# An expert loop with its gathers and additions spread out, and an end with other operations

## The chip, the core and the metric

The kernel runs on one core of a Trainium2 chip. A core has TensorE (matrix products, written PE in the profile, its weight loads PEld), VectorE (DVE), ScalarE (ACT), GpSimd (POOL) and SyncE (SP), which here issues nearly all transfers from the chip's main memory (HBM) into the on-chip memory (SBUF). Matrix products land in eight PSUM banks. Measured is the time of one execution in microseconds (us), the median of several.

## The reference

A two-layer backbone on 256 latent tokens of width 1024 and 256 context tokens. Each layer mixes the tokens in four parallel branches and then applies a channel mixer; in the second layer this is a choice of 2 out of 8 experts, whose weights (8 x 3 matrices of 1024 x 3584 in float32) are most of what is read:

```python
def moe_swiglu(h, router, w1, w3, w2):
    logits = (h @ router).astype(jnp.float32)
    top_v, top_i = lax.top_k(logits, TOP_K)
    probs = jax.nn.softmax(top_v, axis=-1)
    combine = jnp.sum(jax.nn.one_hot(top_i, N_EXPERTS, dtype=jnp.float32) * probs[..., None], axis=-2).astype(h.dtype)
    out = jnp.zeros_like(h)
    for e in range(N_EXPERTS):
        out = out + combine[..., e:e + 1] * swiglu(h, w1[e], w3[e], w2[e])
    return out
# in the layer: x = x + g2 * moe_swiglu(h2, ...), and at the very end
# return rmsnorm(x, final_norm_g)
```

## The kernel before

The first layer and the second layer's mixer take some 815 us; the change touches only what follows, the experts.

**Routing.** `last_proj` finishes the residual `res` in two tiles of 128 tokens; for each, `finish` computes the router's logits `lg` and the normalized tokens `H` in two parts, H1 (rounded to float32r, the fast matmul type) and the remainder H2. `route` ranks the logits and finds each token's place in its expert's list (`pos`); its inner function `weights` makes the softmax weights `comb`. `by_load` sorts the experts by their number of tokens: expert 0 stays first, the three fullest of the others are "heavy" (128 slots, computed with split float32r products: `split` makes two parts of each weight unit, a cast on ScalarE, L145, and a subtraction on VectorE, L146), the other four and expert 0 are "light" (64 slots, plain float32 on the raw weights). It also reads the experts' numbers into SP's registers, for the addresses of their weights.

**Gathering.** `one_hot` builds P from position and choice; `gather` multiplies H by P in eight column blocks (L1058), each evicted by ScalarE and VectorE into XE (heavy) or XL (light), through two PSUM banks of the tag "sm"; `turned` transposes P to PT for the way back. A call serves one heavy and one light expert. For a light expert P and Q hold the one-hots beside zeros, so that PT has 128 rows for each half.

**The loop** in `moe` goes through 56 steps, 21 heavy and 35 light: seven chunks of 512 hidden columns for each expert. The first four steps are light ones of expert 0 (`lead`), then heavy and light ones are mixed evenly. A step reads six weight units of 1 MiB: w1 and w3 in two halves each (`moe_first`, `light_first`) and w2 in two (`moe_second`, `light_second`, called later, after the transpose of the activation, `turns`). Inside a step, between units, stand calls that interleave other work: `look_ahead` splits a coming unit, and `heavy_aside` or `light_aside` run one part of a gather (`run(side, 1)`), the transposes, the second product, or the additions. Within the loop the order of every compute engine is the program's order, written out by a chain of dependencies at the end of `moe`; ahead of it a planner orders the work.

**Adding.** After an expert's last chunk `scatter` or `light_scatter` multiplies the result by the gate `g2`, splits it in two float32r parts Y1 and Y2, and later four `put`s follow: each multiplies PT by Y1 and Y2 (L1208, L1209) and adds the product, times the token's weight, to half a tile of `res` (L1211).

**Buffers.** SP loads units into ten buffers in turn (L119) and waits for each until its last reader is done. With four more units in the split's tiles and three in tiles that are free until later, seventeen are loaded ahead of the loop's first product. `final` normalizes `res` and writes the output.

Of the kernel before, what the change touches and what calls it, by code (L numbers as in the profile page):

```python
# [49 lines left out]
class Net:  # L50
    def __init__(self, tc, d, dump=None):
# [18 lines left out]
        self.hact, self.hpool = (1,), (1,)  # L70
# [873 lines left out]

    def route(self):
# [3 lines left out]
        lg, sel, oh1, oh2 = self.lg, T("sel"), T("oh1"), T("oh2")  # L949
        big = E.tile([128, 2, 2, 8, 8], F32, tag="P", name="big", bufs=1)  # L950
        gt, ge = (big[:, i] for i in range(2))
        selb = E.tile([128, 2, 8], BF16, name="selb")
        rank = T("rank")
        for t in range(2):
            mine = lg[:, t, :, None].to_broadcast([128, 8, 8])
            other = lg[:, t, None, :].to_broadcast([128, 8, 8])
            V.tensor_tensor(ge[:, t], other, mine, op=ALU.is_equal)
            V.tensor_tensor(ge[:, t], ge[:, t], self.low, op=ALU.mult)
            V.tensor_tensor(gt[:, t], other, mine, op=ALU.is_gt)
            V.tensor_tensor(gt[:, t], gt[:, t], ge[:, t], op=ALU.add)  # L960
            V.tensor_reduce(rank[:, t], gt[:, t], axis=AX.X, op=ALU.add)
            V.tensor_scalar(selb[:, t], rank[:, t], 1.5, None, op0=ALU.is_lt)
            V.tensor_scalar(sel[:, t], rank[:, t], 1.5, None, op0=ALU.is_lt)
# [32 lines left out]
        self.comb, self.sel, self.pos, self.tmp = comb, sel, pos, tmp  # L996
        self.dbg("pos", pos)

    def by_load(self):
# [31 lines left out]
        self.placed.append(table("combS", self.comb))  # L1031
# [18 lines left out]
    def gather(self, P, XE=None, XL=None):  # L1050
# [3 lines left out]
        for k in range(8):  # L1054
# [10 lines left out]
            if XL is not None:  # L1065
                nc.scalar.activation(XL[:, k], pg[:, o:], AF.Identity, bias=sh, scale=A)
# [15 lines left out]
    def moe_first(self, src, XE, c, aside=lambda n: None):  # L1082
# [3 lines left out]
        for n, name in enumerate(("m_w1", "m_w3")):  # L1086
            ps = self.bank(tag="mm")
            for kh in range(2):
# [8 lines left out]
                self.look_ahead()  # L1097
                aside(2 * n + kh)
# [89 lines left out]
    def scatter(self, PT, y, cmb):  # L1188
# [16 lines left out]
    def put(self, t, s, PT, Y1, Y2, cmb):  # L1205
        nc = self.nc
        ps = self.bank(tag="mm")
        nc.tensor.matmul(ps, PT, Y1, start=True, stop=False)  # L1208
        nc.tensor.matmul(ps, PT, Y2, start=False, stop=True)  # L1209
# [3 lines left out]
    def light_scatter(self, PT, y, cmb):  # L1213
        nc = self.nc
        Y = self.O.tile([128, 2, 1024], F32R, tag="Y", name=self.nm("Y"))
        Y1, Y2, yg = Y[:, 0, :512], Y[:, 1, :512], self.t2()
        for hf in range(2):
            p = slice(64 * hf, 64 * hf + 64)
            nc.vector.tensor_tensor(yg[p], y[p], self.g2[p, 512 * hf:512 * hf + 512], op=ALU.mult)
# [3 lines left out]
        for t in range(2):  # L1223
            for hf in range(2):
                self.put(t, slice(512 * hf, 512 * hf + 512), PT[:, t, hf], Y1, Y2, cmb)
# [4 lines left out]
    def moe(self):  # L1230
# [3 lines left out]
        def tables(i):  # L1234
            tabs = (self.pos, self.sel, self.comb) if i == 0 else self.placed
            return [a[:, :2, i:i + 1] for a in tabs]

        def light(i, P):

            Q = E.tile([128, 2, 128], F32R, tag="Q", name=self.nm("Q"), bufs=1)  # L1240
            nc.vector.memset(P[:, :, 192:].bitcast(F32), 0.0)
            nc.vector.memset(Q[:, :, :64].bitcast(F32), 0.0)
            pos, sel, _ = tables(i)
            self.one_hot(P[:, :, 128:192], pos, sel)
            self.one_hot(Q[:, :, 64:], pos, sel)
            XE[i] = E.tile([128, 8, LCAP], F32, tag="XL", name=self.nm("XL"), bufs=2)
            PT[i] = E.tile([128, 2, 2, 128], F32R, tag="PTL", name=self.nm("PTL"), bufs=2)
            return Q

        def heavy(i, P):  # L1250
            pos, sel, _ = tables(i)
            self.one_hot(P[:, :, :128], pos, sel)
            XE[i], PT[i] = self.xe_tile(), self.pt_tile()

        def turn(i, P, Q=None):
            if Q is None:
                self.turned(PT[i], [P[:, t, :128] for t in range(2)])
            else:
                self.turned(PT[i].rearrange("p t h c -> p (t h) c"), [x for t in range(2) for x in (P[:, t, 128:], Q[:, t])])

        def gather(i, j):
# [4 lines left out]
            Q = light(j, P)  # L1266
            yield from self.gather(P[:, :, 0 if i else 128:192], XE.get(i), XE[j])
            if i:
                turn(i, P)
            turn(j, P, Q)  # L1270
# [16 lines left out]
        run(side, 9)  # L1287
# [22 lines left out]

        def second(kind, **kw):

            while todo[kind] and todo[kind][0] in G:
# [4 lines left out]
                if c == EFF_CH - 1:  # L1318
                    late.append((self.scatter if kind else self.light_scatter)(PT[i], y[i], tables(i)[2]))
# [15 lines left out]
        for m, (i, c) in enumerate(steps):  # L1335
            kind = big(i)
            if i == 0 and c == 4:
# [3 lines left out]
                nc.scalar.dma_start(self.fg, self.d["fng"])  # L1341
            if c == 0 and i not in ready:
# [4 lines left out]
            def light_aside(n):  # L1347
                if n == 1:
                    turns(False)
                if n == 3 and big(after[0]):  # L1350
# [9 lines left out]
                elif n == 3 and todo[True] and not any(big(x) for x, _ in steps[m:]):  # L1360
# [388 lines left out]
```

## Time and profile before

| | us |
|---|---|
| median of 3 runs | 1694.98 (1692.75 to 1695.25) |
| the profiled execution, time | 1690.82 |
| its span, first to last instruction | 1689.1 |
| busy: TensorE | 1608.9 (95%) |
| busy: VectorE, ScalarE, GpSimd | 955.9, 679.7, 35.4 |
| read from HBM | 478.86 MB |
| mean granted clock of TensorE | 0.976 |

The profile is of one execution. Start times in the rows count from the span's start. Matmuls are pipelined: the duration of one is longer than the distance to the next, and the distance is what a row of them costs. A float32 product appears as two records. The granted clock is a share of the full 2.4 GHz. "Idle before" stands in brackets with what ended it.

### The profile page before, as it was taken

How to read it: one execution, taken by the hardware profiler on the slowest of the kernel's cores; microseconds unless marked ns; L12 is line 12 of the kernel's file. 1: busy time of each engine (PE TensorE's matmuls, PEld its weight loads, DVE VectorE, ACT ScalarE, POOL GpSimd, SP SyncE). 2: the span in 40 equal slices, each digit the busy share in tenths (PEclk: the TensorE clock that was granted, in tenths of full speed). 3: DMA queues.
4: the chain of work that ended last, by engine and by line, in shares of the span. 5: the costliest groups of instructions: out<-in, count | busy, mean ns of one | idle time of the engine just before them, and what ended most of it. 6: DMA issues, size and time to landing. Idle time of an engine off the chain costs nothing. (4 is left out here: it accounts for less than half of the span.)

```text
span 1689.1 us, 23700 instructions
## 1 busy us (share of the span) xinstructions
PE 1608.9 (95%) x9333; PEld 1202.3 (71%) x9333; DVE 955.9 (57%) x1455; ACT 679.7 (40%) x1086; POOL 35.4 (2%) x46
## 2 busy tenths in 40 slices
PE   6999999999999999999899999999999999999986
PEld 3878799887787878999656766666676666775653
DVE  3769655567565688588314554447454454545343
ACT  4654244422222226765314434344343343533341
POOL 1000000000000030000000000000000000000000
PEclk9999999999999999999798999999999999999997
DMA  9544441535443542325898999999999999999994
GB/s 363 195 164 150 180 162 51 184 140 189 160 174 138 207 154 101 125 76 205 335 417 315 419 418 413 405 418 419 418 395 398 419 420 412 418 419 419 419 420 168
DMA packets 69030, 481.55 MB, mean 285 GB/s; under 512 B 8064, under 2 KB 8192, under 8 KB 12336
## 3 DMA queue, kind: packets, MB, share of 16 engines
q1 hardware_dynamic: 68480, 479.43, 71.5%
q8 instruction: 75, 1.23, 0.3%
q10 hardware_dynamic: 432, 0.54, 0.1%
q14 instruction: 43, 0.35, 0.1%
HBM read 478.86 MB, written 1.08 MB: 284 GB/s over the span
## 5 line engine op out<-in xcount | busy, mean ns | idle before, releaser
L146 DVE TENSOR_TENSOR s<-raw,s 128x1024 fp32r<-128x1024 f32 (+1 forms) x350 | 414.9, 1221 | 272.2 <-ACT s L145 271.6
L145 ACT CAST s<-raw 128x1024 fp32r<-128x1024 f32 (+1 forms) x350 | 355.4, 1050 | 277.6 <-PE mm L181 98.0
L176 PE MATMUL mm<-X,s 128*128 128x512 f32 (+1 forms) x672 | 247.2, 368 | 0.0
L181 PE MATMUL mm<-X,s 128*128 128x512 f32 (+1 forms) x672 | 247.0, 368 | 0.0
L182 PE MATMUL mm<-X,s 128*128 128x512 f32 (+1 forms) x672 | 245.8, 368 | 0.0
L1157 PE MATMUL mm<-raw,XL 128*64 128x256 f32 x1952 | 218.9, 380 | 0.6 <-DMA raw<-in_m_w_dram 0.6
L1157 PEld LDWEIGHTS mm<-raw,XL 128*64 128x64 f32 x1952 | 138.7, 137 | 82.6 <-issue 15.9
L176 PEld LDWEIGHTS mm<-X,s 128*128 128x128 f32 x672 | 126.4, 188 | 27.9 <-issue 6.7
L181 PEld LDWEIGHTS mm<-X,s 128*128 128x128 f32 x672 | 126.7, 189 | 26.0 <-issue 5.9
L182 PEld LDWEIGHTS mm<-X,s 128*128 128x128 f32 x672 | 126.6, 189 | 24.0 <-issue 3.4
L176 PE MATMUL mm<-s,XE 128*128 128x512 f32 x336 | 139.2, 414 | 2.2 <-ACT s L145 2.1
L181 PE MATMUL mm<-s,XE 128*128 128x512 f32 x336 | 136.4, 406 | 2.0 <-DVE s L146 2.0
L182 PE MATMUL mm<-s,XE 128*128 128x512 f32 x336 | 135.9, 404 | 0.0
L1184 PE MATMUL yl<-raw,GL 128*64 128x512 f32 x488 | 110.5, 597 | 0.5 <-ACT GL L1172 0.5
L1161 ACT ACTIVATE t<-mm 128x256 f32<-128x256 f32 x35 | 13.5, 386 | 218.9 <-PE mm L1157 218.9
L176 PE MATMUL mm<-s,X 128*128 128x256 f32 (+1 forms) x304 | 86.5, 287 | 2.0 <-ACT mix L666 2.0
L181 PE MATMUL mm<-s,X 128*128 128x256 f32 (+1 forms) x304 | 86.0, 285 | 0.8 <-DVE s L146 0.8
L1163 DVE TENSOR_TENSOR t<-t,mm 128x256 f32<-128x256 f32 x35 | 14.6, 417 | 125.0 <-PE mm L1157 124.9
L182 PE MATMUL mm<-s,X 128*128 128x256 f32 (+1 forms) x304 | 85.1, 285 | 0.0
L1184 PEld LDWEIGHTS yl<-raw,GL 128*64 128x64 f32 x488 | 33.0, 137 | 63.6 <-issue 62.0
L176 PEld LDWEIGHTS mm<-s,XE 128*128 128x128 f32 x336 | 65.6, 195 | 17.3 <-ACT s L145 3.1
L181 PEld LDWEIGHTS mm<-s,XE 128*128 128x128 f32 x336 | 65.5, 195 | 17.4 <-DVE s L146 3.1
(384 smaller groups left out, 2347.7 us busy)
## 6 DMA issues: line engine op xcount, KB each, us to landing
raw<-in_m_w_dram SPq DMA_DIRECT2D x294, 1024.0 KB, 14.0
mraw<-in_mod_w_dram SPq DMA_DIRECT2D x47, 1024.0 KB, 4.9
raw<-in_f_w_dram SPq DMA_DIRECT2D x33, 1024.0 KB, 5.0
mraw<-in_m_w_dram SPq DMA_DIRECT2D x32, 1024.0 KB, 12.4
raw<-in_w_in_dram SPq DMA_DIRECT2D x20, 1024.0 KB, 4.8
raw<-in_w_out_dram SPq DMA_DIRECT2D x8, 1024.0 KB, 5.6
first<-in_m_w_dram SPq DMA_DIRECT2D x8, 512.0 KB, 9.0
once<-in_m_w_dram SPq DMA_DIRECT2D x3, 1024.0 KB, 16.1
```

What stands on the lines that cost most here:

```text
L145: self.last = (nc.scalar.copy(s1[:, :h], r), nc.vector.tensor_tensor(s2[:, :h], r, s1[:, :h].bitcast(F32), op=ALU.subtract))
L146: nc.vector.tensor_tensor(s2[:, :h], r, s1[:, :h].bitcast(F32), op=ALU.subtract))
L176: m = mm(out, a[0], b[0], start=first, stop=False)
L181: self.keep(mm(out, a[0], b[1], start=False, stop=False))
L182: self.keep(mm(out, a[1], b[0], start=False, stop=last))
L1157: self.keep(nc.tensor.matmul(ps[64 * b:64 * b + 64], XL[:, k], w(o, o + 256), start=(k == 0), stop=(k == 7), tile_position=(0, 64 * b)))
L1161: nc.scalar.activation(g, ps, AF.Silu)
L1163: self.keep(nc.vector.tensor_tensor(g, g, ps, op=ALU.mult))
L1184: self.keep(self.nc.tensor.matmul(y[64 * hf:64 * hf + 64], G[:, b, 64 * hb:64 * hb + 64], w(o, o + 512), start=(c == 0 and hb == b == 0), ...
```

## The change

1. `rank_of` is cut out of `route` and called in `finish` for each tile of tokens as its logits are there; the subtraction for H2 of the second tile goes from GpSimd to VectorE (`hpool`).
2. `weights` and the table of the sorted weights, `combS`, move from ahead of the loop into its second step.
3. A gather now first makes its one-hots and yields; ahead of the loop these are made for experts 1 and 4 too, and the eight parts of that gather run in light steps 1 to 3, three per step. Later gathers make their one-hots as soon as they are set up. In the first gather every second eviction goes to VectorE.
4. For light experts P holds the one-hots twice and Q is gone; the additions use 64 rows of the array (`tile_position`) for each half.
5. `heavy_aside` does one `put` per call in place of four in two calls; in `moe_first` the aside goes ahead of `look_ahead`, but for the second.
6. After the last heavy step its transposes and additions move into the first half of the next light step.
7. The light gate is laid out in `g2l` and applied in one multiplication; the last expert's additions take the result in float32, without the split.
8. `final` multiplies by the norm's weight ahead of the scale, so that after the root one operation remains.

```diff
-        self.hact, self.hpool = (1,), (1,)
+        self.hact, self.hpool = (1,), ()
...
             if XL is not None:
-                nc.scalar.activation(XL[:, k], pg[:, o:], AF.Identity, bias=sh, scale=A)
+                if o == 0 and k % 2:
+                    nc.vector.tensor_scalar(XL[:, k], pg, A, sh, op0=ALU.mult, op1=ALU.add)
+                else:
+                    nc.scalar.activation(XL[:, k], pg[:, o:], AF.Identity, bias=sh, scale=A)
...
-                self.look_ahead()
-                aside(2 * n + kh)
+                if 2 * n + kh == 1:
+                    self.look_ahead()
+                    aside(1)
+                else:
+                    aside(2 * n + kh)
+                    self.look_ahead()
...
-                self.put(t, s, PT[:, t], Y1[:, s], Y2[:, s], cmb)
+                self.put(t, s, PT[:, t], (Y1[:, s], Y2[:, s]), cmb)
+                yield
...
+        yg = self.t2()
+        nc.vector.tensor_tensor(yg, y, self.g2l, op=ALU.mult)
+        if last:
+            for t in range(2):
+                for hf in range(2):
+                    p = slice(64 * hf, 64 * hf + 64)
+                    self.put(t, slice(512 * hf, 512 * hf + 512), PT[p, t].bitcast(F32), (yg[p],), cmb, tile_position=(64 * hf, 0))
+            return
...
         def gather(i, j):
             P = E.tile([128, 2, 256], F32R, tag="P", name=self.nm("P"), bufs=1)
             if i:
                 heavy(i, P)
-            Q = light(j, P)
+            light(j, P)
+            yield
...
         def begin():
             yield from gather(None, 0)
-            self.weights()
             self.by_load()
-            yield
             yield from gather(1, NH + 1)
...
-        run(side, 9)
+        run(side, 10)
...
         def heavy_aside(n):
             if n == 1:
                 turns(False)
-                puts()
+                put()
                 second(True, aside=lambda: run(side, 1))
-            elif n == 3:
-                puts()
+            else:
+                put()
             run(side, 1)
...
+            if i == 0 and c == 1:
+                self.weights()
+                self.combS = self.table("combS", self.comb)
...
-            def light_aside(n):
-                if n == 1:
+            def light_aside(k):
+                if k == 1:
                     turns(False)
-                if n == 3 and big(after[0]):
+                    if not any(big(x) for x, _ in steps[m:]):
+                        turns(True)
+                        puts()
+                    if 0 < m < n:
+                        run(side, 3)
+                if k == 3 and big(after[0]):
...
                 side = gather(*more[i, c])
+                run(side, 1)
...
+            r = self.rms(ss, t)
+            for hf in range(2):
+                s = slice(512 * hf, 512 * hf + 512)
+                nc.vector.tensor_tensor(both[:, t, s], self.res[t][:, s], self.fg[:, s], op=ALU.mult)
             for hf in range(2):
...
-                if self.fmode and hf < self.fmode:
-                    nc.scalar.activation(o, self.res[t][:, s], AF.Copy, scale=rt)
-                    nc.vector.tensor_tensor(o, o, self.fg[:, s], op=ALU.mult)
+                if hf == 0:
+                    nc.scalar.activation(o, o, AF.Copy, scale=r)
                 else:
-                    nc.vector.scalar_tensor_tensor(o, self.res[t][:, s], rt, self.fg[:, s], op0=ALU.mult, op1=ALU.mult)
+                    nc.vector.tensor_scalar(o, o, r, None, op0=ALU.mult)
```

## Rows read from the trace of the kernel before

**Rows 1.** The page, transfer rate (GB/s) in 40 slices of the span.
```profile
GB/s 363 195 164 150 180 162 51 184 140 189 160 174 138 207 154 101 125 76 205 335 417 315 419 418 413 405 418 419 418 395 398 419 420 412 418 419 419 419 420 168
```

**Rows 2.** By stretches: length, busy us per engine, granted clock, transfer share, GB/s.
```profile
828.00:1672.00 844.00, 803.60 (x4680) 537.70 (x4678) 388.24 (x459) 324.86 (x442) 0.00 (x0) 0.97 0.98 401
832.00:848.00 16.00, 16.00 (x130) 9.39 (x128) 0.84 (x2) 1.04 (x3) 0.00 (x0) 0.97 0.63 235
888.00:920.00 32.00, 29.31 (x148) 18.39 (x150) 12.38 (x15) 13.15 (x20) 0.00 (x0) 0.85 0.76 280
1040.00:1440.00 400.00, 382.59 (x2234) 262.05 (x2233) 201.41 (x242) 164.63 (x226) 0.00 (x0) 0.98 1.00 411
1440.00:1660.00 220.00, 208.51 (x1181) 138.41 (x1181) 99.49 (x101) 83.82 (x105) 0.00 (x0) 0.98 1.01 419
1660.00:1664.00 4.00, 4.00 (x40) 2.70 (x38) 0.00 (x0) 0.38 (x1) 0.00 (x0) 1.00 0.37 146
```

**Rows 3.** Timeline ahead of the loop: start, us, engine, line, out<-in, count [idle before].
```profile
814.95 0.23 DVE L1586 SCALAR_TENSOR_TENSOR lg<-sm,rstd,shR 128x8 f32<-128x8 f32 x1 [0.77 <-PE sm L1608]
...
816.26 2.49 POOL L1596 TENSOR_TENSOR H<-t,H 128x512 fp32r<-128x512 f32 x2 [1.45 <-ACT t L1592]
...
816.52 1.03 DVE L962 TENSOR_SCALAR selb<-rank 128x8 bf16<-128x8 f32 x1
...
819.72 2.84 PE L1058 MATMUL sm<-P,H 128*128 128x64 f32 x12 [0.67 <-DVE P L1047]
...
821.46 1.28 ACT L977 ACT_TABLE_LOAD   x1
...
828.63 9.28 PE L1157 MATMUL mm<-first,XL 128*64 128x256 f32 x64
...
839.68 0.33 SPq L119 DMA_DIRECT2D mraw<-in_m_w_dram  x1
```

**Rows 4.** Timeline of TensorE, gather of experts 1 and 4, first heavy chunk.
```profile
879.91 1.14 PE L1058 MATMUL sm<-P,H 128*128 128x192 f32 x8
...
892.97 0.79 PE L176 MATMUL mm<-s,XE 128*128 128x512 f32 x1 [1.62 <-ACT s L145]
...
895.25 0.63 PE L176 MATMUL mm<-s,XE 128*128 128x512 f32 x1
895.67 0.63 PE L181 MATMUL mm<-s,XE 128*128 128x512 f32 x1
...
898.54 0.39 PE L176 MATMUL mm<-s,XE 128*128 128x512 f32 x1
898.77 0.40 PE L181 MATMUL mm<-s,XE 128*128 128x512 f32 x1
```

**Rows 5.** Waits, 905 to 1660: engine, line <- releaser: us, times, longest.
```profile
PE mm L1208 <- DVE res L1211: 12.2, 4, 3.1
...
PE sm L1058 <- DVE P L1047: 9.7, 3, 3.4
...
PE y L176 <- ACT G L1120: 5.0, 1, 5.0
...
PE sm L1073 <- ACT XL L1066: 4.6, 2, 2.3
```

**Rows 6.** Timeline, two float32 products of 512 columns.
```profile
870.43 1.98 PE L365 MATMUL mod<-mrow,ident 128*128 128x512 f32 x4
```

**Rows 7.** Timeline of the end.
```profile
1641.00 1.99 ACT L145 CAST s<-raw 128x1024 fp32r<-128x1024 f32 x2 [4.69 <-DMA raw<-in_m_w_dram]
...
1672.60 1.39 DVE L1219 TENSOR_TENSOR t<-yl,gf 64x512 f32<-64x512 f32 x2 [3.19 <-PE yl L1184]
...
1676.01 3.07 DVE L1211 SCALAR_TENSOR_TENSOR res<-mm,combS,res 128x512 f32<-128x512 f32 x4 [0.59 <-PE mm L1209]
...
1681.95 0.72 ACT L1662 ACTIVATE out<-res,rstd 128x512 f32<-128x512 f32 x1 [1.17 <-POOLq L1403]
...
1682.70 0.69 DVE L1663 TENSOR_TENSOR out<-out,gf 128x512 f32<-128x512 f32 x1
```

More of the change, by code (lines that the diff above doesn't have):

```diff
@@ L942, in ffn, with rank_of @@
         second(DFF_CH - 1, prev)
+    def rank_of(self, t):
+        nc, V, lg = self.nc, self.nc.vector, self.lg
+        gt, ge = (self.t2((128, 8, 8), tag="t1") for _ in range(2))
+        mine = lg[:, t, :, None].to_broadcast([128, 8, 8])
+        other = lg[:, t, None, :].to_broadcast([128, 8, 8])
+        V.tensor_tensor(ge, other, mine, op=ALU.is_equal)
+        V.tensor_tensor(ge, ge, self.low, op=ALU.mult)
+        V.tensor_tensor(gt, other, mine, op=ALU.is_gt)
+        V.tensor_tensor(gt, gt, ge, op=ALU.add)
+        V.tensor_reduce(self.rank[:, t], gt, axis=AX.X, op=ALU.add)
+        V.tensor_scalar(self.selb[:, t], self.rank[:, t], 1.5, None, op0=ALU.is_lt)
+        V.tensor_scalar(self.sel[:, t], self.rank[:, t], 1.5, None, op0=ALU.is_lt)
     def route(self):
@@ L948, in route @@
         T = lambda nm, *sh: E.tile([128, 2, 8, *sh], F32, name=nm)
[L949 to L963, printed above, removed]
+        lg, sel, selb, rank, oh1, oh2 = self.lg, self.sel, self.selb, self.rank, T("oh1"), T("oh2")
         m = E.tile([128, 4, 2], F32, name="mx")
@@ L1202, in scatter, with put, light_scatter @@
                 s = slice(512 * hf, 512 * hf + 512)
-                self.put(t, s, PT[:, t], Y1[:, s], Y2[:, s], cmb)
-    def put(self, t, s, PT, Y1, Y2, cmb):
+                self.put(t, s, PT[:, t], (Y1[:, s], Y2[:, s]), cmb)
+                yield
+    def put(self, t, s, PT, Y, cmb, **kw):
         nc = self.nc
         ps = self.bank(tag="mm")
-        nc.tensor.matmul(ps, PT, Y1, start=True, stop=False)
-        nc.tensor.matmul(ps, PT, Y2, start=False, stop=True)
+        for i, y in enumerate(Y):
+            nc.tensor.matmul(ps, PT, y, start=(i == 0), stop=(i == len(Y) - 1), **kw)
         a = self.res[t][:, s]
         nc.vector.scalar_tensor_tensor(a, ps, cmb[:, t], a, op0=ALU.mult, op1=ALU.add)
-    def light_scatter(self, PT, y, cmb):
+    def light_scatter(self, PT, y, cmb, last=False):
         nc = self.nc
+        yg = self.t2()
[6 more added lines that the diff above has]
+            return
         Y = self.O.tile([128, 2, 1024], F32R, tag="Y", name=self.nm("Y"))
[L1216 to L1219, printed above, removed]
+        Y1, Y2 = Y[:, 0, :512], Y[:, 1, :512]
         nc.scalar.copy(Y1, yg)
@@ L1224, in light_scatter @@
             for hf in range(2):
-                self.put(t, slice(512 * hf, 512 * hf + 512), PT[:, t, hf], Y1, Y2, cmb)
+                p = slice(64 * hf, 64 * hf + 64)
+                self.put(t, slice(512 * hf, 512 * hf + 512), PT[p, t], (Y1[p], Y2[p]), cmb, tile_position=(64 * hf, 0))
+                yield
     def ys(self):
@@ L1309, in puts, with put @@
                 run(late.pop(0))
+        def put():
+            if late and next(late[0], self) is self:
+                late.pop(0)
         def second(kind, **kw):
@@ L1318, in second @@
                 if c == EFF_CH - 1:
+                    puts()
+                    if kw.get("last"):
+                        run(self.light_scatter(PT[i], y[i], tables(i)[2], True))
+                        return
                     late.append((self.scatter if kind else self.light_scatter)(PT[i], y[i], tables(i)[2]))
@@ L1341, in moe @@
                 nc.scalar.dma_start(self.fg, self.d["fng"])
+                self.g2l = E.tile([128, 512], F32, name="g2l")
+                for hf in range(2):
+                    nc.scalar.copy(self.g2l[64 * hf:64 * hf + 64], self.g2[64 * hf:64 * hf + 64, 512 * hf:512 * hf + 512])
             if c == 0 and i not in ready:
@@ L1359, in light_aside @@
                         self.plan[2:2] = [(source(i)("m_w2", c, hb), 1) for hb in range(2)]
-                elif n == 3 and todo[True] and not any(big(x) for x, _ in steps[m:]):
+                elif k == 3 and todo[True] and not any(big(x) for x, _ in steps[m:]):
                     i, c = todo[True][0]
                     self.plan = [(source(i)("m_w2", c, hb), 1) for hb in range(2)]
-                if n == 3:
+                if k == 3:
                     for _ in range(2):
@@ L1572, in last_proj @@
         tc, nc, sh, RA, shR = self.tc, self.nc, self.modc[:, 3, 0], self.RA, self.shR
-        self.lg = self.C.tile([128, 2, 8], F32, name="lg")
+        self.lg, self.rank, self.sel = (self.C.tile([128, 2, 8], F32, name=n) for n in ("lg", "rank", "sel"))
+        self.selb = self.C.tile([128, 2, 8], BF16, name="selb")
         lgp = [self.bank((128, 8), tag="sm") for _ in range(2)]
@@ L1653, in final @@
                 self.sq(ss, t, hf, self.res[t][:, 512 * hf:512 * hf + 512])
-            if self.fseq:
-                r.append(self.rms(ss, t))
-        for t in range(2):
-            rt = r[t] if self.fseq else self.rms(ss, t)
+            r = self.rms(ss, t)
+            for hf in range(2):
+                s = slice(512 * hf, 512 * hf + 512)
+                nc.vector.tensor_tensor(both[:, t, s], self.res[t][:, s], self.fg[:, s], op=ALU.mult)
             for hf in range(2):
```

38 lines of the change are left out of this document (17 added, 21 removed).

## The prediction

> **What bounds the kernel now.** I read the page's line of transfer rates first [rows 1]. Over the first half the rate is far below its ceiling; from slice 20 on it stands at about 419 GB/s and falls only here and there. That second half is the experts' loop. Its weights are 8 x 7 x 6 = 336 units of 1 MiB, 352 MB, which at 419 GB/s take 841 us. So in the loop a microsecond can be won in three places only: where the transfers break off, behind the last transfer, and not at all on an engine that merely keeps pace.
>
> Next I asked for the breaks by stretches [rows 2]. Against the 419 GB/s of 1440 to 1660, the stretch 832 to 848 moved 235: 16 x (1 - 235/419) = 7.0 us lost. 888 to 920 lost 32 x (1 - 280/419) = 10.6 us, and 1040 to 1440, in five places, 400 x (1 - 411/419) = 7.6 us. Together 25.2 us. After 1440 there is none. The transfers end at 1660 + 4 x 146/419 = 1661.4, and the program runs on to 1689.1: a tail of 27.7 us.
>
> Why do they break off? SP fills every buffer and then waits until TensorE has read one: the load after the fill goes out at 839.68, two us after the preloaded weights' 64 matmuls end [rows 3]. So a break is TensorE being all buffers behind. The third view is therefore the waits of TensorE in the loop [rows 5]: 12.2 us on the residual's additions, 9.7 us on the one-hots P, 4.6 us before a transpose, 5.0 us once for a cast of G. From 828 to 1672 TensorE is busy 803.6 of 844 us at a mean clock of 0.97 [rows 2]; it idles 40.4 us, and 3% of 844 = 25 us more go to the low one of its two clocks, which follows the stands (1.2 instead of 2.4 GHz): after the stand that ends at 892.97, matmuls of 512 columns start 0.42 us apart, at 898.5 they start 0.23 apart [rows 4]. Without both its work is some 780 us, less than the 841 of the transfers. TensorE, then, is not the bound by its work, only by its stands.
>
> **The change part by part.**
>
> (a) *Ahead of the loop.* From the second logits at 814.95 to the first gather matmul at 819.72 are 4.8 us [rows 3]. In it VectorE ranks both row tiles, and one small comparison takes 1.03 us while GpSimd's two subtractions (2.49 us) run. After: the first tile is ranked earlier, when its own logits are there, and the subtractions go to VectorE (two of about 0.7 us, waiting for ScalarE anyway). I take 2.2 us off. The softmax leaves the gather: its table load (1.28 us [rows 3]) stood between the gather's evictions; 0.7 us off, as the two banks hide the rest. Two transposes fewer at the low clock, 0.4 us. Sum 3.3 us; bounds 0 (the order here is the planner's, and the subtractions may land in the chain) and 4.7. The first break then lasts 3.7 us rather than 7.0.
>
> (b) *The gather of experts 1 and 4.* Before, it stands alone: from 879.91 TensorE does nothing else until the first heavy matmul at 892.97, 13.1 us, and then some eleven matmuls at the low clock, 11 x 0.19 = 2.1 us [rows 4]. After, its nine parts go three at a time into light steps 1 to 3. It issues no transfers. In a batch two parts find a free bank, the third waits for an eviction; behind that wait queue the light step's own matmuls, and behind these SP for their buffers. Alone a part costs 13.1/9 = 1.45 us; I take 0.9, for the batches start with free banks: 8.2 us in all (bounds 4.6 and 13.1). TensorE reaches the first heavy chunk 13.1 + 2.1 - 8.2 = 7.0 us earlier, with (a) 10.3. The transfers can give back at most 17.6 less the 3.7 that remain and up to 2.5 of new holding back in step 1, that is 11.4. TensorE's 10.3 is the smaller: (a) and (b) together 10.3 us, bounds 2 (0 and 2.1) and 15 (17.6 less the 2.3 that remain when (a) gives 4.7).
>
> (c) *The loop's breaks, 7.6 us.* They follow the stands of rows 5. The additions came four in a row, with three banks, behind VectorE's splits; now one per stop. The one-hots were issued with the gather that reads them; now a step earlier. Evictions went behind the next split; now ahead of it in three stops of four. What is late next is that split: an addition of 0.77 us (4 in 3.07 [rows 7]) goes ahead of it, 32 in the loop, 25 us of VectorE; with it VectorE has 388 of 844 us to do [rows 2], so mostly covered. TensorE had to be late by all ten buffers for a break, so small new waits cost nothing. I take 7.0 back; bounds 0 and 7.6.
>
> (d) *The tail to the last expert product.* ScalarE waits 4.69 us for the transfer at 1641.00 [rows 7]: TensorE follows the data here. It ends at 1672.6 [rows 7], 11.2 us behind the last byte. The 5.0 us stand for G [rows 5] goes, since the transposes move ahead of the splits that blocked the cast; the heavy additions (8 matmuls x 0.23 = 1.9 us) move under the last transfers; the low clock after the stand gives about 2. That is 8.9, but the data limits it: one unit of 2.5 us and its eight matmuls (1.8) must follow, so at best 11.2 - 4.3 = 6.9. The heavy chunk's second split still comes first; I take 5, bounds 2 and 6.9.
>
> (e) *The end.* From 1672.60 the first addition starts 3.4 us later, at 1676.01, and the four end at 1679.08 [rows 7]. After: one multiplication (0.7) and then float32 matmuls at once. A float32 product of 512 columns is two records of 0.45 us (4 in 1.98 [rows 6]): the first addition can start at 1.9 us, the last product is there at 0.8 + 4 x 0.9 + 0.2 = 4.6, the last addition ends at 5.3 rather than 6.5: 1.2 less. At the low clock it is twice as long, and the last addition ends at 8.6: 2.1 more. The norm's last two operations, 0.72 and 0.69 us in a row [rows 7], become one: 0.7 less; the small reductions no longer queue behind a scaling: 0.6. Sum 2.5; bounds -0.8 and 3.7. TensorE has stood for under a microsecond by then, so I take the high clock.
> The Trainium skill (TensorE: Matmul & The Clock Gate, Part 3 on packing) says that matmuls on different row groups run at the same time. No row here shows two halves of 64 rows; by that rule the four products take 1.8 instead of 3.6 us, the additions themselves set the pace, and the sum would be 0.5 us larger.
>
> *At nothing:* the softmax and its table load in light step 1 (ScalarE is busy 1.0 of 16 us there, VectorE 0.8 [rows 2]; without that cover up to 2 x 1.28 us); two ScalarE copies of the gate; doubled one-hots in place of two memsets; additions from 64 rows, which stream the same 512 columns. SP keeps its order, and the read of the experts' numbers still ends well ahead of 839.68.
>
> **Sum:** 10.3 + 7.0 + 5 + 2.5 = 24.8 us. The profiled execution took 1690.82 us (span 1689.1), so it would be 1666.0. The median before, 1694.98, lies 4.2 above it; I carry the difference over: **1670 us**. With every lower bound (2 + 0 + 2 - 0.8) it is 1692, with every upper one (15 + 7.6 + 6.9 + 3.7) 1662; the case's own range, without the ends that all need to meet, is 1664 to 1678.
>
> **The rivals.**
> 1. *The front only moves its break.* The batches hold the light steps back as long as the gather did, and TensorE arrives no earlier. Then (a) and (b) give 3.3, and with TensorE as late as before half of (c) stays: 3.3 + 3.5 + 3 + 1.5 = 11.3, 1684 us. For it: eight parts in a row took 13.1 us because of evictions, which stay. Against: TensorE ran ahead of the transfers in 848 to 888. Chance 0.17.
> 2. *All breaks close.* TensorE gains ground in the light steps, so even the first break shrinks, and the tail is as short as data allow: 25.2 - 2 + 6.9 + 3.7 = 33.8, 1661 us. For it: no break after 1440, where there were still stands. Chance 0.12.
> 3. *Slower: the splits become late.* Place: the 32 stops of the loop at which an addition now goes ahead of a split on VectorE. TensorE has the 40 + 25 = 65 us of rows 2 to lose before it is as slow as now, so it decides from 65/32 = 2.0 us per stop. If each cost the 2.3 us of a transpose's wait (4.6 for two [rows 5]) that is 74 us, and a low clock (2 us) after every third adds 21: 95 - 65 - 7 (tail) = 23 us more, 1718. Against: the addition is 0.77 us. Chance 0.06.
> 4. *It does not do what it says:* the stands only change place. Within 0.2%, 1694. Chance 0.04.
>
> The forecast has 0.61. Faster by over 0.2% (3.4 us, about what a measurement of this kernel tells from no change): 0.61 + 0.17 + 0.12 = 0.90; within: 0.04; slower: 0.06. The range that holds 8 of 10 takes the forecast's range, most of rival 2 and half of rival 1: 1659 to 1685.
>
> **What would show it.** Right: the first light matmul about 3 us earlier; no stretch of gather matmuls alone ahead of the first heavy chunk and the rate near 419 from there to the end; the waits of rows 5 gone; transfers ending near 1644 on this clock; about 6 us from the last byte to the last expert product; 8 us from there to the last scaling. Wrong: a break of several us in light steps 1 to 3; new waits of TensorE on the splits with the low clock behind; float32 records 0.9 us apart at the end.

## The result and the profile after

The changed kernel takes 1671.06 us (median; 1670.76 to 1672.62) against 1694.24 of the kernel before beside it (1692.75 to 1695.25): a ratio of 0.9873, 95% interval 0.986 to 0.9885. Forecast were 1670, from 1659 to 1685. The profiled execution took 1670.76 us (span 1669.0), that of before 1690.82: from profile to profile the change is worth 20.1 us where the sum said 24.8. The forecast of the time came closer than its sum by luck: the 4.2 us carried over from the profile to the median made up for most of what the sum had too much.

The page's transfer rates in 40 slices of the span of the changed kernel answer to [rows 1]. The dips of the loop (413, 405, 395, 398, 412) are gone; one is left, at 371 and 339 in slices 20 and 21.
```profile
GB/s 362 195 173 152 156 191 52 171 134 175 154 212 137 174 183 124 102 101 122 371 339 418 420 420 421 420 421 421 420 421 420 421 420 421 420 421 421 421 420 192
```
By stretches, with the columns of [rows 2]:
```profile
832.00:848.00 16.00, 15.40 (x124) 9.20 (x122) 5.25 (x23) 5.90 (x12) 0.00 (x0) 1.00 0.66 247
...
864.00:880.00 16.00, 14.69 (x98) 7.71 (x96) 1.74 (x5) 5.10 (x12) 0.00 (x0) 1.00 0.85 318
888.00:920.00 32.00, 32.00 (x179) 21.17 (x178) 14.99 (x17) 13.53 (x18) 0.00 (x0) 1.00 1.01 421
1040.00:1440.00 400.00, 387.07 (x2248) 259.63 (x2246) 202.01 (x234) 165.50 (x223) 0.00 (x0) 1.00 1.01 421
```
And the stretch in which the transfers end:
```profile
1632.00:1648.00 16.00, 15.82 (x102) 8.99 (x100) 5.47 (x9) 1.99 (x4) 0.00 (x0) 1.00 0.75 305
```
Read as the prediction read them, against the 421 GB/s that is now the full rate: 832 to 848 loses 16 x (1 - 247/421) = 6.6 us (7.0 before), 864 to 880 loses 3.9 (none before), 888 to 920 nothing (10.6 before). The front's breaks are 10.5 us instead of 17.6. In the loop no break is left, and the rate is 421 where before it was 411 with and 419 without breaks. Counted at the full rate the transfers end at 1632 + 16 x 305/421 = 1643.6 instead of 1661.4 (forecast 1644): 17.8 us, 7.1 of them from the front and 10.7 from there to 1632. But the last transfers ebb instead of ending at once, so this count runs ahead of what has landed. A landing that the program waits for is the last heavy unit that ScalarE splits, at 1641.00 in [rows 7]:
```profile
1625.18 1.99 ACT L145 CAST s<-raw 128x1024 fp32r<-128x1024 f32 x2 [3.62 <-DMA raw<-in_m_w_dram]
```
By it the transfers gained 15.8 us: 7.1 in the front and, as the rest, 8.7 in the loop.

The front in TensorE's timeline (columns of [rows 3]):
```profile
817.11 0.17 PE L991 MATMUL sm<-selb,SU 128*128 128x8 bf16 x1 [2.06 <-DVE selb L956]
...
818.67 7.11 PE L1058 MATMUL sm<-P,H 128*128 128x64 f32 x32 [1.34 <-DVE P L1047]
...
826.21 3.25 PE L1164 MATMUL mm<-first,XL 128*64 128x256 f32 x14
...
885.20 0.50 PE L176 MATMUL mm<-s,XE 128*128 128x512 f32 x1
```
VectorE between the two records of 817.11 and 818.67:
```profile
817.48 0.69 DVE L1630 TENSOR_TENSOR H<-t,H 128x512 fp32r<-128x512 f32 x1 [0.35 <-ACT t L1626]
818.09 0.18 DVE L995 COPY pos<-sm 128x24 f32<-128x24 f32 x1
```
The first light matmul comes 2.4 us earlier than in [rows 3]. The first heavy matmul comes at 885.20 (892.97 in [rows 4]) and no gather stands alone ahead of it. SP's issues in between show where the transfers stop:
```profile
838.58 0.33 SPq L119 DMA_DIRECT2D raw<-in_m_w_dram  x1
838.96 0.42 SPq L107 DMA_DIRECT2D once<-in_m_w_dram  x1
843.23 15.35 SPq L119 DMA_DIRECT2D raw<-in_m_w_dram  x8
865.11 0.34 SPq L119 DMA_DIRECT2D mraw<-in_m_w_dram  x1
870.66 15.52 SPq L119 DMA_DIRECT2D raw<-in_m_w_dram  x9
```
Two things stand in these rows that no one had asked for. Between 865.11 and 870.66 SP issues nothing: light step 3 holds its buffers that long. And the load "once" (line 107) goes out at 838.96; in the kernel before, all three of these went out from 813.80 on:
```profile
813.80 1.50 SPq L107 DMA_DIRECT2D once<-in_m_w_dram  x3
```
The planner has put one of them behind the reads of the expert numbers, so that 16 instead of 17 units are asked for ahead of the light steps.

The waits of TensorE from 888 to 1616 (columns of [rows 5]):
```profile
PE mm L176 <- ACT s L145: 4.6, 5, 1.1
PE mm L181 <- DVE s L146: 3.8, 5, 0.8
PE sm L1058 <- DVE P L1047: 3.8, 3, 2.0
PE sm L1076 <- ACT XL L1069: 3.6, 2, 1.8
PE mm L1164 <- DMA raw<-in_m_w_dram: 2.7, 7, 0.4
```
The stands on the residual's additions (12.2 us) are gone, those on one-hots and the evictions shrank, and the short ones on the splits (lines 176 and 181) grew from 4.1 us in five to 8.4 us in ten. The last line is what matters: TensorE's products now wait for data. The same view of the kernel before holds no such line for PE in that stretch.

The end on VectorE, ScalarE and SP (columns of [rows 7]); the last expert product ends at 1652.96 (1672.6 before):
```profile
1654.92 0.75 DVE L1219 SCALAR_TENSOR_TENSOR res<-mm,combS,res 128x512 f32<-128x512 f32 x1 [1.22 <-PE mm L1217]
1655.71 0.69 DVE L1690 TENSOR_TENSOR out<-res,gf 128x512 f32<-128x512 f32 x1
1656.32 1.40 DVE L1219 SCALAR_TENSOR_TENSOR res<-mm,combS,res 128x512 f32<-128x512 f32 x2
1657.64 0.68 DVE L1690 TENSOR_TENSOR out<-res,gf 128x512 f32<-128x512 f32 x1
1658.24 0.74 DVE L1219 SCALAR_TENSOR_TENSOR res<-mm,combS,res 128x512 f32<-128x512 f32 x1
...
1660.16 0.15 DVE L384 TENSOR_REDUCE rstd<-ss 128x1 f32<-128x2 f32 x1
```
```profile
1661.12 1.33 ACT L1695 ACTIVATE out<-out,rstd 128x512 f32<-128x512 f32 x2 [1.33 <-POOL rstd L240]
```
```profile
1661.64 1.81 SPq L1698 DMA_DIRECT2D out_dram<-out  x4
```
The weight's multiplications (line 1690) stand between the additions. From the last product to the last scaling (1662.45) are 9.5 us instead of 10.8; but all four outputs now leave together, and from there to the end of the span are 6.55 us instead of 5.7. The end is worth 0.5 us.

### The profile page after: what moved, and what is told of

The parts are those of the page before. It is cut to its first block, busy times and chain, and to the rows that moved or that the text cites. A ratio compares the mean times of both kernels' runs of the same rounds, so it can differ in the third digit from the quotient of the medians.

```text
span 1669.0 us, 23655 instructions
## 1 busy us (share of the span) xinstructions
PE 1602.7 (96%) x9323; PEld 1188.6 (71%) x9323; DVE 954.6 (57%) x1451; ACT 676.8 (41%) x1079; POOL 32.5 (2%) x44
## 4 chain that ended last, share of the span: by engine, by line
PE 75%; DMA 14%; DVE 6%; ACT 3%; issue 1%; SPq 0%; POOL 0%; ACTq 0%; DVEq 0%; POOLq 0%
PE mm L176 16%; PE mm L181 16%; PE mm L182 16%; DMA raw<-in_m_w_dram 12%; PE mm L1164 9%; PE yl L1191 5%; DVE s L146 4%; ACT s L145 1%; PE y L181 1%; PE y L182 1%; PE y L176 1%; DMA raw<-in_mod_w_dram 1%; PE sm L1058 1%; PE mod L253 1%; PE mm L1217 1%
## 5 line engine op out<-in xcount | busy, mean ns | idle before, releaser
L176 PEld LDWEIGHTS mm<-s,XE 128*128 128x128 f32 x336 | 64.2, 191 | 22.5 <-ACT s L145 5.8
L181 PEld LDWEIGHTS mm<-s,XE 128*128 128x128 f32 x336 | 64.4, 192 | 19.6 <-DVE s L146 5.8
L182 PEld LDWEIGHTS mm<-s,XE 128*128 128x128 f32 x336 | 64.3, 191 | 15.1
```

What stands on the lines that cost most here:

```text
L176: m = mm(out, a[0], b[0], start=first, stop=False)
L181: self.keep(mm(out, a[0], b[1], start=False, stop=False))
L182: self.keep(mm(out, a[1], b[0], start=False, stop=last))
```

## The experiments

All runs compare with the kernel before on their own chip, whose median was 1691.2 to 1692.6 there; so the ratios are to be compared with the changed kernel's 0.9873, not the microseconds. Their intervals reach 0.1 to 0.17% to either side. "The change" below is the changed kernel.

**1. All 17 units ahead again.** The early loads are traced and queued in the order of their use before the expert numbers are read:
```
+ for c in range(1, 4):
+     for name, cc in (("m_w1", c), ("m_w3", c), ("m_w2", c - 1)):
+         for kh in range(2):      # 13 units, each behind the one before
+             firsts.append(raw_unit(d[name][0, cc, kh]))
  side = begin()
```


> The changed kernel with its 13 early loads of the shared expert traced in one piece ahead of the load of the expert numbers and queued in the order of their use, so that all 17 units (not 16) are asked for before SP waits for the expert numbers. Theory A (the unit that slipped behind the expert numbers is what the front lost): transfers run one unit, 1 MiB or 2.5 us at 420 GB/s, further before they stop, the breaks at 828 to 880 us fall from 10.5 us to about 8, and the time falls by 2.5 us to about 1668.5. Rival B (the breaks come from the gather's work between the light steps' matmuls, and another unit only moves them later): the break moves to the next light step and the time stays within 0.5 us of 1671.

Measured: 1671.05 us, ratio 0.988 (0.9865 to 0.9895). The stretches say why nothing came of it:
```profile
832.00:848.00 16.00, 15.40 (x124) 9.24 (x122) 5.25 (x23) 6.16 (x12) 0.00 (x0) 1.00 0.80 302
864.00:880.00 16.00, 14.70 (x100) 7.71 (x98) 1.74 (x5) 5.10 (x12) 0.00 (x0) 1.00 0.75 268
```
The first break fell from 6.6 to 4.5 us, the second grew from 3.9 to 5.8. Rival B: the unit moves the break. What counts is the moment at which TensorE last holds all buffers, not how many units were ahead.

**2. The kernel before with 16 units ahead.**
```
- self.nonce = 3
+ self.nonce = 2
```


> The kernel before with two instead of three early buffers, so 16 units ahead instead of 17, nothing else. Theory A: 2.5 us slower than before (about 1696.7), with all of it in a longer break at 832 to 848 us. Rival B: the lone gather behind the fourth light step gives the slack that a missing unit would need, the time is that of before within 0.5 us.

Measured: 1691.5 us, ratio 0.9997 (0.9987 to 1.0006). Rival B again, and on the other front. My first suspicion, the load that slipped, is ruled out from both sides.

**3. The gather alone again.** 
```
- if 0 < m < n:
-     run(side, 3)
```


> The changed kernel with the first heavy expert's gather taken out of light steps 1 to 3: it runs alone before the first heavy chunk, as before. In this order the third early unit is asked for ahead of the expert numbers again. Theory A (placing the gather is worth its PE time less the breaks that it causes): first heavy chunk some 5 us later than in the changed kernel, a break of 5 to 7 us at 885 to 905 us as before, but 2.5 us less of a break at 830 to 848 and none at 864 to 880 (3.9 us): the two cancel to within 2 us, 1670 to 1673. Rival B (placing it is worth the whole 7 us that the forecast gave, and the third unit nothing): 1676 to 1678.

Measured: 1674.63 us, ratio 0.9899 (0.9884 to 0.9914), that is 0.0026 or 4.4 us above the change, between the two theories. Its stretches:
```profile
832.00:848.00 16.00, 16.00 (x134) 9.18 (x132) 3.32 (x17) 3.20 (x5) 0.00 (x0) 1.00 0.85 324
864.00:880.00 16.00, 14.71 (x100) 7.90 (x96) 1.90 (x6) 4.47 (x10) 0.00 (x0) 1.00 1.02 421
888.00:920.00 32.00, 30.42 (x161) 19.50 (x162) 15.25 (x15) 14.18 (x18) 0.00 (x0) 0.91 0.79 297
```
The breaks are 3.7 + 9.4 us, with 0.6 at 880 to 888 (390 GB/s) 13.7 in all, against 10.5: 3.2 us, near what was timed. The first heavy matmul comes at 889.12, 3.9 us later than in the change. So this is what moving the gather is worth, not 7.0.

**4. Another order at the end.**
```
- ps = bank("mm")                            # all four additions
+ ps = bank("mm" if t + hf < 2 else "sm")    # the fourth in another bank
- for t in 0, 1: both[t] = res[t] * fg; out[t] = both[t] * r[t]
+ both[1] = res[1] * fg                      # behind the last addition
+ out[0] = (res[0] * r[0]) * fg              # one VectorE instruction a half
+ out[1] = both[1] * r[1]                    # ScalarE
```


> The changed kernel with another order at the end: the four additions of the last expert in a row (the fourth into another bank), norm's weight multiplied ahead only for the second 128 tokens, behind the last addition, the first 128 tokens scaled in one instruction each on VectorE, the second on ScalarE. Theory A (the multiplications between the additions cost the end what it was to gain): last addition 1.2 us earlier, last scaling 1 to 1.5 us earlier, the first outputs leave earlier, time 1 to 2 us less, 1669 to 1670. Rival B (the reductions' own chain, or the output transfers behind one another, set the end): within 0.5 us of 1671.

Measured: 1671.05 us, ratio 0.9875 (0.986 to 0.989). Rival B, by an order that I hadn't foreseen. VectorE, three rows of its timeline:
```profile
1659.04 0.15 DVE L384 TENSOR_REDUCE rstd<-ss 128x1 f32<-128x2 f32 x1 [0.19 <-ACT t L380]
1659.12 0.75 DVE L1219 SCALAR_TENSOR_TENSOR res<-sm,combS,res 128x512 f32<-128x512 f32 x1
...
1661.71 0.15 DVE L384 TENSOR_REDUCE rstd<-ss 128x1 f32<-128x2 f32 x1
```
The first sum stood ahead of the last addition and the second behind a scaling. The last addition ended 5.0 us behind the last product (1654.82) instead of 6.0, but the last scaling 9.8 behind it instead of 9.5.

**5. The old loop in the change.** Split first and the rest after it in each quarter, additions in fours, one-hots traced with the gather's first part:
```
- if 2 * n + kh == 1: look_ahead(); aside(1)
- else: aside(2 * n + kh); look_ahead()
+ look_ahead(); aside(2 * n + kh)
- put()            # one half at each stop
+ puts()           # all four, at stops 1 and 3
```


> The changed kernel with the old order in the heavy chunks: the look-ahead split ahead of what is done beside it in all four quarters, additions of four halves in a row, one-hots traced with the gather's first part. All else as changed. Theory A (the loop's breaks are worth what the rate of 1040 to 1440 us showed, and nothing makes up for them later): 411 instead of 421 GB/s in that stretch, one-hot stands of 9 to 10 us again, 7 to 9 us slower than the changed kernel, 1678 to 1680. Rival B (with PE ahead of the data after the front, half of the breaks are covered by its lead): 3 to 4 us, 1674 to 1675.

Measured: 1672.52 us, ratio 0.9894 (0.9877 to 0.991): 1.5 us above the change by the medians, 3.6 by the ratios, whose intervals overlap. The longest of TensorE's waits from 888 to 1616, and a stretch:
```profile
PE mm L1213 <- DVE res L1215: 13.0, 4, 3.3
```
```profile
1040.00:1440.00 400.00, 387.14 (x2242) 263.27 (x2240) 202.13 (x236) 167.13 (x225) 0.00 (x0) 0.98 1.01 420
```
The stands on the additions are back in full (12.2 us before), and the rate does not fall; by the ratios the time is Rival B's. But the other stands of [rows 5] did not come back: the view of the waits holds no line for the one-hots, and ahead of the transposes only 0.5 us. And in the kernel before, the breaks opened behind those others. TensorE's stands and the rates there:
```profile
995.71 0.50 PE L1208 MATMUL mm<-Y,PTL 128*128 128x512 f32 x1 [3.06 <-DVE res L1211]
...
1029.92 0.71 PE L1058 MATMUL sm<-P,H 128*128 128x192 f32 x4 [3.42 <-DVE P L1047]
```
```profile
1000.00:1020.00 20.00, 20.00 (x109) 12.07 (x109) 5.25 (x5) 3.44 (x5) 0.00 (x0) 0.99 1.01 419
1020.00:1040.00 20.00, 16.58 (x88) 12.64 (x85) 13.49 (x21) 11.85 (x16) 0.00 (x0) 0.91 1.01 419
1040.00:1060.00 20.00, 20.00 (x138) 13.49 (x138) 7.08 (x14) 5.28 (x11) 0.00 (x0) 1.00 1.00 402
```
The stand on the additions, which ends at 995.71, leaves the rate at 419; the first break comes behind the one on the one-hots, which ends at 1029.92. So this run shows that 13.0 us of stands on the additions open no break on the new front. Whether that front would cover the old loop with all its stands, no run shows.

**6. The old end in the change.**
```
- yg[p] with PT[p, t].bitcast(F32): float32 products, then res * fg ahead of the scale
+ Y1, Y2 split as in the loop; then the sums; then res * r, * fg
```


> The changed kernel with the old end: last expert's rows split into two parts and added by 64-row float32r products, norm's scale and weight in the old order behind the sums. Theory A (the new end is worth the 0.5 us that the two traces differ by: 1.3 us to the last scaling less 0.8 us on the outputs): 1671 to 1672. Rival B (it is worth the 2.5 us of the forecast): 1673.5.

Measured: 1670.6 us, ratio 0.9882 (0.9866 to 0.9899). Theory A: step (e) is worth nothing that can be timed.

**7. The last heavy chunk's transposes and additions back behind the last light step.**
```
- if not any(big(x) for x, _ in steps[m:]):
-     turns(True); puts()      # beside quarter 1
+ turns(True)                  # behind the step
```


> The changed kernel with the last heavy chunk's transposes and the waiting additions put back behind the last light step instead of beside its second quarter. Theory A (this is the 3.4 us by which the last product moved closer to the last byte): the last expert product comes 11 us behind the last byte instead of 7.8, 1674 to 1675. Rival B (the move only takes PE time from one side of the step to the other; the 3.4 us came with the additions' order in the loop): within 0.7 us of 1671.

Measured: 1675.18 us, ratio 0.9903 (0.9886 to 0.9919), 4 to 5 us above the change; Theory A. TensorE's longest wait from 1600 to 1665 is the one of [rows 5] again:
```profile
PE y L176 <- ACT G L1127: 5.0, 1, 5.0
```
In the change the longest there is 1.7 us.

**8. The gather in single parts.**
```
- if k == 1 and 0 < m < n: run(side, 3)
+ if 0 < m < n: run(side, 1)      # at every quarter
```


> The changed kernel with the first heavy expert's gather in single parts beside each quarter of light steps 1 to 3 instead of three parts beside the second quarter. Theory A (PE sets the front, so the 2.3 us that it stands for evictions inside the batches of three are what the break at 864 to 880 us costs): stands gone, rate there 350 GB/s or more, first heavy chunk 1.5 to 2.3 us earlier, 1669. Rival B (single parts stand for their own evictions just as long, or another wait takes their place): within 0.7 us of 1671.

Measured: 1670.04 us, ratio 0.9878 (0.9862 to 0.9895). The trace is that of Theory A: TensorE busy 16.00 of 16 us in all three stretches of the light steps, 352 GB/s at 864 to 880, the first heavy matmul at 883.41, 1.8 us earlier, a span of 1667.3. In the times the gain is below what can be told.

**9. The new loop alone, on the old front.** In the kernel before:
```
- look_ahead(); aside(2 * n + kh)
+ if 2 * n + kh == 1: look_ahead(); aside(1)
+ else: aside(2 * n + kh); look_ahead()
- puts()
+ put()
  side = gather(*more[i, c])
+ run(side, 1)     # the one-hots, a step ahead
```

> The kernel before with the new order in the heavy chunks alone (split after what is done beside it in three of four quarters, additions one half at a time, one-hots ahead); its front and its end are the old ones. Theory A (the stands of the loop cost only while PE has no lead on the data; the old front leaves it none, so here the stands' removal pays in full): 1040 to 1440 us at 419 GB/s or more instead of 411, 6 to 8 us faster than before, 1684 to 1686. Rival B (as undoing the loop's part of the changed kernel cost 1.5 us only, the part is worth 1 to 2 us on either front): 1690.

Measured: 1685.49 us, ratio 0.9962 (0.995 to 0.9975): 6.4 us faster, Theory A.
```profile
1040.00:1440.00 400.00, 383.22 (x2254) 260.16 (x2251) 202.90 (x237) 168.22 (x229) 0.00 (x0) 1.00 1.01 419
```
The breaks of the loop close on the old front too, and TensorE waits for data (3.3 us from 888 to 1616). So the loop's order closes the loop's breaks by itself. (The profiled execution, 1682.43, was the fastest of five; the others took 1684.77 to 1686.77.) By the ratios, the 6.4 us here and the 17.9 us that are left without the loop's order in 5 make 24.3, against 21.5 for both together. The two parts may share some 3 us, but the intervals of the three ratios together are wider than that, and 5 kept a part of the loop's gain.

**10. Unread products in TensorE's stands ahead of the gather.** In the change's trace the granted clock falls from 1.00 to 0.50 in the stands at 816 us and is back at 1.00 at 830; the gather runs at half speed between.
```
+ for _ in range(n):      # n = 2, 8, 5 in the three stands
+     matmul(unread, ident, ident)
```


> The changed kernel with 15 products of the identity with itself, 128 columns each, whose results nobody reads, in PE's three stands between 813 and 819 us (2, 8 and 5 of them). Theory A (PE's clock, which fell to 0.50 at 815.7 us in those stands and rose again at 829, is what the front waits for): granted clock 1.00 from 812 to 832, the shared expert's gather takes 3.6 to 4.5 us instead of 7.2, the first light product comes 2.5 to 3.5 us earlier, the breaks at 832 to 880 us shrink by as much or more (another 1.2 us from the light products at half clock), time 1666.5 to 1668.5. Rival B (the clock falls all the same, or the gather's pace is set by its evictions): gather 6 us or more, time within 0.7 us of 1671; where the products run at half clock they delay the counts by up to 1.5 us, 1672.5.

Measured: 1671.11 us, ratio 0.9873 (0.9858 to 0.9887). The gather and the first light matmul:
```profile
822.05 1.05 PE L1066 MATMUL sm<-P,H 128*128 128x64 f32 x8
823.26 4.45 PE L1066 MATMUL sm<-P,H 128*128 128x64 f32 x24 [0.16 <-ACT XL L1077]
...
828.14 2.40 PE L1172 MATMUL mm<-first,XL 128*64 128x256 f32 x10
```
Everything up to here came some 3 us later in this execution. The stands were filled and the clock stayed at 1.00 to 824, but then it fell, inside the gather. It took 5.7 us instead of 7.1; the breaks came to 5.0 + 0.3 + 3.5 = 8.8 us instead of 10.5. In the times it does not show: Rival B there, and between the theories in the trace.

**11. All together:** 1, 8 and 10, the end of 4 in a forced order, the gathered rows' subtractions behind the ranks, and the last heavy expert's four additions spread over the waits of the last light step:
```
- puts()                              # beside quarter 1 of the last light step
+ put()
- puts(); turns(False); second(False, last=True)
+ put(); turns(False); put(); second(False, last=True)   # the fourth in its end
```

> The changed kernel with these together: 15 unread products that fill PE's stands ahead of the gather; the second half of the gathered rows' differences behind the ranks on VectorE; 17 units ahead; the first heavy gather in single parts; the last heavy expert's four additions spread over the waits of the last light step (one beside its second quarter, one ahead of and one behind the transposes, one behind the last products); the end with four additions in a row, the fourth in another bank, first sum, weight of the second 128 tokens, second sum, then the scalings. Theory A (the parts add up: front 3 to 4 us, last product 1.5 us closer to the last byte, last scaling 1.5 us closer to the last product): 1663 to 1666. Rival B (what the front gains is lost where the transfers then become the bound, and the tail keeps its length behind the last byte): 1669 to 1671.

Measured: 1666.58 us, ratio 0.9853 (0.9839 to 0.9867); on the same chip as 10, 4.5 us less, and between the two theories. It is the fastest kernel of the study together with the next. Last product at 1650.37, last scaling at 1659.19. TensorE, rows of the front and of the end:
```profile
816.88 3.55 PE L964 MATMUL y<-ident 128*128 128x128 f32 x16 [0.67 <-DVE lg L1643]
...
822.68 3.38 PE L1067 MATMUL sm<-P,H 128*128 128x64 f32 x24 [0.16 <-ACT XL L1078]
...
1652.56 0.59 PE L1230 MATMUL mm<-t,PTL 64*128 64x512 f32 x1
1652.57 0.59 PE L1230 MATMUL sm<-t,PTL 64*128 64x512 f32 x1
```
The unread products waited for their bank, ran at half clock and came out some 2 us too long for their stand; behind them the gather ran at full clock.

**12. The same with fewer of those products and in another bank.**
```
- warm(x, 8, bank("y0"))
- warm(x, 5, bank("y1"))
+ warm(x, 5, pp[:, 24:])
+ warm(x, 4, bank("y1"))
```

> The kernel with everything together, with three changes of what its trace showed: the first unread products write to a bank that doesn't wait for the logits (5 and 4 products instead of 8 and 5, so that they fit the stands even at half clock), only the second half of the rows has its differences behind the ranks (the first half's had moved ahead of the second logits), and at the end the second sum stands between the two weight multiplications. Theory A (in the kernel before this one the gather came 2 us late, behind unread products at half clock): first light product 1.5 to 2 us earlier, breaks at 832 to 880 us 6.5 us in all instead of 8.3, last scaling 0.4 us earlier, time 1664 to 1665. Rival B (the clock falls in the stands all the same and the gather runs at half speed again): first light product as before within 0.5 us, time 1666 to 1667.5.

Measured: 1667.38 us, ratio 0.9852 (0.9836 to 0.9869), no difference from 11: Rival B. TensorE:
```profile
819.96 1.05 PE L1068 MATMUL sm<-P,H 128*128 128x64 f32 x8 [0.81 <-DVE P L1057]
821.16 4.44 PE L1068 MATMUL sm<-P,H 128*128 128x64 f32 x24 [0.16 <-ACT XL L1079]
```
The gather started 1.5 us earlier than in 11 and lost it at half clock: the granted clock fell at 823 us. What the filling bought was one or the other.

## Why the prediction was right, and where its sum was not

What bounds the kernel was read rightly: the transfers do, and a microsecond is won where they break off or behind them. The sum of 24.8 against the 20.1 of the two profiles: (a) and (b) were to give 10.3 and gave 7.1, (c) 7.0 and 8.7, (d) 5 and 3.8, (e) 2.5 and 0.5, with the transfers counted to the landing of the last heavy unit. One by one:

- **(a)** forecast 3.3, measured 2.4 on the first light matmul. The risk that the text named was there: a subtraction on VectorE (817.48) stood ahead of the positions' copy (818.09).
- **(b)** forecast 7.0; experiment 3 gives 3.2 in the breaks and 4.4 in the times. This is the step that was mis-sized most. TensorE's own part came as forecast: the first heavy matmul comes 7.8 us earlier, where (a) as measured and the text's 13.1 - 8.2 make 7.3, and no low clock follows it (1.00 from 888 to 920). What failed is the next step, that the transfers get back as much as TensorE gains. The text let the batches hold the transfers back in light step 1 only. Light step 3 does it too: the new break of 3.9 us at 864 to 880, listed under "wrong: a break of several us in light steps 1 to 3". Without the batches, in experiment 3, the rate there is 421. Behind the new break the rate is 419 or more, so that what TensorE gained beyond it was worth nothing to the transfers. With (a) the front's breaks closed by 7.1 us instead of 10.3. So the mechanism of rival 1, a front that moves its break, took 3.2 of the 10.3.
- **(c)** forecast 7.0, at most 7.6. Counted at the full rate 10.7 came, of which 7.6 are the breaks and about 3.1 the full rate itself, 421 instead of 419; by the landing of the last heavy unit it was 8.7; the difference lies in the ebb at the end. The mechanism is right: experiment 9 closes the breaks with the loop's order alone. Whether (b) and (c) in part pay for the same breaks stays open. Experiment 5 fits a lead of TensorE from the new front that pays for the stands on the additions; it fits as well that these stands alone open no break, as at 995.71 in the kernel before.
- **(d)** forecast 5. From 11.2 us behind the last byte to 9.4, counted at the full rate, is 1.8. From the landing of the last heavy unit, where the ebb (305 GB/s from 1632 on) does not enter, to the last product it is 27.8 us (1625.18 to 1652.96) instead of 31.6 (1641.00 to 1672.6), 3.8 less. Undoing the move costs 4 to 5 us (7), and 32.4 us by the same measure, so the mechanism is right: the 5.0 us stand for G is gone. A stand of 1.7 us for a split, with the low clock behind it, took part of its place, as the text said a split would.
- **(e)** forecast 2.5, measured 0.5, and nothing in the times (6). The additions began on time, 2.0 us behind the last product. But the norm's multiplications came between them, so that the last ended at 6.0 instead of 5.3; the sums came behind those; and the outputs, which before left in turn, left together. Moving work ahead of a scale helps only if it is not also ahead of the last addition.
- **The Trainium skill** (TensorE: Matmul & The Clock Gate, Part 3 on packing) was weighed at (e): products on different row groups run at the same time. The traces agree: in experiment 11 two records of 64 rows start at 1652.56 and 1652.57, and all eight lie within 2.0 us, near the 1.8 of the rule and not the 3.6 of my sum. In the changed kernel the eight take 3.09 us from 1653.76 on. It did not help, for VectorE set the pace.
- **At nothing:** the softmax's table loads, the gate's copies and the additions from 64 rows left no break in light step 1 beyond those above. SP did not keep its order (the third early load), which the text had taken for granted; 1 and 2 show that this cost nothing.
- **Rival 3** (splits late) has its sign in the waits, 8.4 us in ten stands, none over 1.1, with a mean clock of 1.00 and the full rate from 1040 to 1440: covered.

Left open: why the full rate is 419 GB/s on the old front, in experiment 9 too, and 420 to 421 on the new; why the last transfers ebb; and whether the new front would cover the old loop with all its stands.

## What to carry to other kernels

Stands of an engine that has slack over the transfers are not to be added up: a break appears only when the engine is all buffers behind, and 13.0 us of stands in experiment 5 opened none. For the same reason an engine that arrives earlier does not hand all of its gain to the transfers: ask where the moved work will hold the buffers now, and price the break that opens there against the one that closes. Where a stream of transfers ebbs, measure it at a landing that the program waits for. And the last microseconds want the chain from the last operand written out as a whole, the outputs with it: an operation moved ahead of one wait often stands in another.

## What the runs showed of the hardware

The granted clock fell while TensorE's rows were full. In experiment 12 it is 1.00 from 812 to 820, where TensorE is busy 6.28 of 8 us, and 0.68 from 820 to 828, where it is busy 7.79 of 8: it fell to 0.50 at 823, inside the gather's products of 64 columns. The stands of TensorE ahead of that were 0.81 us, up to 819.96, and 0.16 us. In experiment 11 the same products, behind 3.6 us of unread ones of 128 columns at half clock, ran at full clock; it fell to 0.50 behind them, at 827.

One more unit of transfers ahead (0.988 against 0.9873, within the intervals, in experiment 1), or one less (0.9997 in experiment 2), changed nothing that can be told, though each is 2.5 us of transfer.
